# Two transformer mixers on one core: the projections as plain f32 products, without the split into fp32r halves

## The chip, the core and the metric

The kernel runs as one program on one of the eight cores of a Trainium2 chip. The metric is the device time of one execution in microseconds (us), lower being better. A core has four engines that matter here: TensorE (PE; its weight loads are listed apart as PEld), VectorE (DVE), ScalarE (ACT) and GpSimd (POOL). The queue of SyncE (SP) issues the loads from HBM, and 16 DMA engines carry them out.

## What is computed

Two transformer blocks run one after the other on 256 tokens of width 1024, all in f32. Each block is a mixer and then a mixture of experts. Cut to the lines that matter:

```
# block 1
proj = rms_norm(x, g_mix) @ w_in                      # 1024 x 5432
ya = gla_mixer(...) @ w_br_gla ;  yb = dsa_mixer(...) @ w_br_att
x = x + (sigmoid(gate_a) * ya + sigmoid(gate_b) * yb) @ w_out
x = x + hier_moe(rms_norm(x, g_ffn), ...)             # 32 experts, width 128
# block 2
proj = rmsnorm(x, norm_mix_2) @ w_in_2                # 1024 x 3080
x = x + concat(rmsnorm(forgetting), rmsnorm(dilated)) @ w_out_2
x = x + hierarchical_moe(...)                         # 32 experts, width 512
```

The experts are picked by the largest router logits, so the products that feed the routers need more digits than one fp32r product gives.

## The kernel before

**Stages.** Mixer 1 (0 to about 228 us) is followed by routing and experts of block 1 (to about 338 us), mixer 2 (to about 490 us) and the experts of block 2 (to the end at 959.4 us). The 256 tokens are two tiles of 128 (`NT = 2`, `tt`). Activations are turned to 128 features by 256 tokens once for each mixer (`to_feat`, L325).

**Weights.** Every weight tile is 128 x 4096 f32, 2 MB, loaded by SP into one of several slots (`wload`, `stream_tile`). A slot is filled again when its last reader is done. Five slots exist from the start and others are opened as memory comes free; the experts have 9 in block 1 and 10 in block 2. So the first 9 or 10 expert tiles can be loaded ahead of the routing, and no more.

**Projections.** `project` (L298) loads 1024 rows of up to 512 columns and calls `gemm_tok` (L280): for each of 8 steps of 128 rows (`k`) it multiplies both token tiles with that slice of weights, into an accumulator `acc` (PSUM, 4 banks). `gemm_feat` (L290) does the same the other way round for the four gate projections: the weights stand in the array and the 256 tokens stream, four products a step. `mixed` (L737), `out_step` (L752) and `out_part` (L1222) are the output projections.

**The split.** Each operand x of such a product is held as two fp32r tiles, hi = x rounded to fp32r and lo = x - hi. `split` (L252) makes both for a slice of weights: ACT writes hi (`whi`, L263), then DVE or POOL in turn writes lo (`wlo`, L264). `products` (L267) issues three matmuls for each product: hi*hi, hi*lo, lo*hi, all of them on L269. The activations' halves are made where they are turned: `to_feat` (L325: `aT_hi` by ACT, `aT_lo` by DVE), `feat_split` (L374), and L749/L750 in `mixed`.

```
with tc.high_priority(offset=SPLIT_AHEAD):
    turn[1] = nc.scalar.activation(r[0], v, AF.Copy)
    eng.tensor_sub(r[1], v, r[0].bitcast(F32))
```

**Order.** No order is written out by hand: a list scheduler places the instructions on each engine by their dependences and priorities, and each engine then runs its list strictly in that order. `SPLIT_AHEAD` raises the priority of the splits. A later projection's matmuls are placed between an attention's matmuls where the scheduler sees a gap.

**Other names.** `head_norm` (L345) normalizes the heads of a projection (ACT L343 and L351, DVE L352, L307 to L313, L355). `pairs_T` (L358) turns them by transposes on PE (L365) and scales on DVE (L369, L371). `rope` (L1124) comes between the two in mixer 2 (POOL L1132, DVE L1134, L1135). L436 and L443 are transposes and products of attention. L571 is a plain f32 product of 128x128 with 128x512, called four times; L623 is one of 128x128 with 128x256, called twice. L541 to L551 find each token's 64 largest index scores on DVE (the mask chain). In names such as `b`, `t4` tiles are meant.

Of the kernel before, what the change touches and what calls it, by code (L numbers as in the profile page):

```python
# [20 lines left out]
P = 128  # L21
T = 256
# [6 lines left out]
SPLIT_AHEAD = 30  # L29
SPLIT_ENGINES = ('vp', 'pv')  # L30
# [106 lines left out]
def two_blocks(ctx: ExitStack, tc: tile.TileContext, A: dict, at: dict, out: bass.AP):  # L137
# [112 lines left out]
    turn = [0, None, 0]  # L250

    def split(v):  # L252
        n = 1
        for c in v.shape[1:]:
            n *= c
        r = []
        for tag in ("whi", "wlo"):
            t = wtile([P, 512], F32R, tag=tag, bufs=4)[:, :n]
            r.append(t if len(v.shape) == 2 else t.rearrange("p (k n) -> p k n", n=v.shape[2]))
        turn[0] += 1  # L260
        eng = nc.gpsimd if SPLIT_ENGINES[turn[2]][turn[0] % 2] == "p" else nc.vector
        with tc.high_priority(offset=SPLIT_AHEAD):
            turn[1] = nc.scalar.activation(r[0], v, AF.Copy)  # L263
            eng.tensor_sub(r[1], v, r[0].bitcast(F32))  # L264
        return r

    def products(todo):  # L267
        def mm(out_, a, b, start, stop, kw):
            nc.tensor.matmul(out_, a, b, start=start, stop=stop, **kw)  # L269

        for out_, (ah, al), (bh, bl), split_a, first, last, kw in todo:
            mm(out_, ah, bh, first, False, kw)
            mm(out_, *((ah, bl) if split_a else (al, bh)), False, False, kw)
        for out_, (ah, al), (bh, bl), split_a, first, last, kw in todo:
            mm(out_, *((al, bh) if split_a else (ah, bl)), False, last, kw)

# [3 lines left out]
    def gemm_tok(ws, hT, accs, then=None):  # L280
        for k in range(8):
            if then is not None and k == then[0]:
                with tc.issue_after(turn[1].ins):
                    then[1]()
            for w, ac in zip(ws, accs):
                wh, wl = split(w[:, k, :])
                products([(ac[tt][:, :w.shape[2]], [h[:, k, tok(tt)] for h in hT], (wh, wl), False, k == 0, k == 7, {})
                          for tt in range(NT)])

    def gemm_feat(w, hT, accs):  # L290
        for k in range(8):
            wh, wl = split(w[:, k, :])
            sl = [slice(b * P, (b + 1) * P) for b in range(4)]
            products([(accs[b // 2][:, (b % 2) * T:(b % 2 + 1) * T], (wh[:, sl[b]], wl[:, sl[b]]),
                       [h[:, k, :] for h in hT], True, k == 0 and b % 2 == 0, k == 7, {"skip_group_check": True})
                      for b in range(4)])

    def project(src, c0, ns, hT, then=None, step=8):  # L298
        ws = [wload(src, 0, 8, c0 + sum(ns[:i]), n, step) for i, n in enumerate(ns)]
        ac = [[acc() for _ in range(NT)] for _ in ns]  # L300
        gemm_tok(ws, hT, ac, then)
        return ac if len(ns) > 1 else ac[0]
# [22 lines left out]
    def to_feat(g):  # L325
        hi = wtile([P, 8, T], F32R, tag="aT_hi", bufs=1, level="inner")
        lo = wtile([P, 8, T], F32R, tag="aT_lo", bufs=1, level="inner")
# [12 lines left out]
        return hi, lo  # L340
# [33 lines left out]
    def feat_split(src, dst, tt, g):  # L374
# [4 lines left out]
        h, l = (d[:, :, tok(tt)] for d in dst)  # L379
        if g is None:  # L380
            nc.scalar.activation(h, v, AF.Copy)
            nc.vector.tensor_sub(l, v, h.bitcast(F32))
        elif g.shape[1] == 1:
            scaled(h, v, g)
            nc.vector.scalar_tensor_tensor(l, v, g, h.bitcast(F32), op0=OP.mult, op1=OP.subtract)
        else:
            for k in range(4):
                gk = g[:, k:k + 1]
                scaled(h[:, k], v[:, k], gk)
                nc.vector.scalar_tensor_tensor(l[:, k], v[:, k], gk, h[:, k].bitcast(F32),  # L390
                                               op0=OP.mult, op1=OP.subtract)
# [117 lines left out]
    gemm_tok([w], hT, [a2], (5, lambda: token_rstd(r_)))  # L509
# [160 lines left out]
    glaT = [t4([P, 4, T], F32R) for _ in range(2)]  # L670
# [39 lines left out]
    for c in range(4):  # L710
# [16 lines left out]
    mh, ml = stream_tile(F32R).rearrange("p (i k t) -> i p k t", i=2, k=8)  # L727
# [9 lines left out]
    def mixed(b):  # L737
        ps = bank()
        s = slice(b * P, (b + 1) * P)
        for i, (w, src) in enumerate(((wg, glaT), (wa, attT))):  # L740
            wh, wl = split(w[:, :, s])
            products([(ps[:, i * T:(i + 1) * T], (wh[:, k, :], wl[:, k, :]), [x[:, k, :] for x in src],
                       True, k == 0, k == 3, {}) for k in range(4)])
        mm = wtile([P, 2, T], tag="on", bufs=2, level="const")
        m = mm[:, 0]
# [356 lines left out]
    turn[2] = 1  # L1102
# [35 lines left out]
    kb = project(w_in2, 2048, [512], hT, (3, lambda: token_rstd(r_)), 4)  # L1138
# [15 lines left out]
    dilT = [t4([P, 4, T], F32R) for _ in range(2)]  # L1154
    dss = wtile([P, NT], tag="dss", bufs=2)

    def out_branch(on, dst, ss, tt, g):
        junk = wtile([P, 512], tag="sq", bufs=2, level="const")
        feat_split(on, dst, tt, g)
# [59 lines left out]
    foxT = [wtile([P, 4, T], F32R, tag="foxT", bufs=2) for _ in range(2)]  # L1219
    fss = wtile([P, NT], tag="dss", bufs=2)  # L1220

    def out_part(w, src, tts):  # L1222
        xo = {(tt, c): acc() for tt in tts for c in range(2)}
        for c in range(2):
            for k in range(4):
                wh, wl = split(w[:, k, c * 512:(c + 1) * 512])
                products([(xo[tt, c], [x[:, k, tok(tt)] for x in src], (wh, wl), False, k == 0, k == 3, {})
                          for tt in tts])
# [51 lines left out]
```

## Time and profile before

| | |
|---|---|
| three timed runs | 960.49, 962.53 (median), 964.93 us |
| span of the profiled execution (first to last instruction) | 959.4 us |
| PE, PEld busy | 754.1, 477.6 us |
| DVE, ACT, POOL busy | 367.8, 271.9, 170.5 us |
| moved by DMA | 304.69 MB, mean 318 GB/s |
| splits of weights: ACT L263, POOL L264, DVE L264 | 120.0, 134.3, 80.8 us busy |

The profiled execution is a run of its own and its own device time isn't given beside its span; the median of the timed runs lies 3.1 us above the span, which is the work around the first and the last instruction. PE's busy time is no measure of a rate, since matmuls are pipelined: one recorded as 0.39 us may be followed by the next 0.23 us later. So prices are taken from starts, not from durations.

### The profile page before, as it was taken

How to read it: one execution, taken by the hardware profiler on the slowest of the kernel's cores; microseconds unless marked ns; L12 is line 12 of the kernel's file. 1: busy time of each engine (PE TensorE's matmuls, PEld its weight loads, DVE VectorE, ACT ScalarE, POOL GpSimd, SP SyncE). 2: the span in 40 equal slices, each digit the busy share in tenths (PEclk: the TensorE clock that was granted, in tenths of full speed). 3: DMA queues.
4: the chain of work that ended last, by engine and by line, in shares of the span. 5: the costliest groups of instructions: out<-in, count | busy, mean ns of one | idle time of the engine just before them, and what ended most of it. 6: DMA issues, size and time to landing. Idle time of an engine off the chain costs nothing. (4 is left out here: it accounts for less than half of the span.)

```text
span 959.4 us, 13937 instructions
## 1 busy us (share of the span) xinstructions
PE 754.1 (79%) x5662; PEld 477.6 (50%) x5662; DVE 367.8 (38%) x788; ACT 271.9 (28%) x617; POOL 170.5 (18%) x158
## 2 busy tenths in 40 slices
PE   7999999998979997988999756555566585655565
PEld 6778899976657576676863313111222141221212
DVE  4966374565435488676561102010010020100201
ACT  6556555552111274665641000000000000000000
POOL 3422344571000056322420000000000000000001
PEclk9899999999989999999999989889787878898967
DMA  9663453684999983624669999999999999999997
GB/s 342 228 225 130 150 192 146 264 350 177 362 406 409 380 305 104 254 89 180 234 252 411 409 409 410 409 409 409 357 409 410 409 409 410 409 409 409 409 382 240
DMA packets 97782, 304.69 MB, mean 318 GB/s; under 512 B 2920, under 2 KB 19048, under 8 KB 97712
## 3 DMA queue, kind: packets, MB, share of 16 engines
q1 hardware_dynamic: 97136, 302.68, 81.6%
q8 instruction: 48, 0.79, 0.3%
q0 software_dynamic: 288, 0.79, 0.2%
q10 hardware_dynamic: 288, 0.26, 0.1%
q14 instruction: 22, 0.18, 0.1%
HBM read 302.65 MB, written 1.06 MB: 317 GB/s over the span
## 5 line engine op out<-in xcount | busy, mean ns | idle before, releaser
L1079 PE MATMUL acc<-w,XT 128*32 128x128 f32 (+1 forms) x2048 | 185.6, 492 | 85.1 <-DMA w<-w_up 47.4
L264 POOL TENSOR_TENSOR wlo<-w,whi 128x512 fp32r<-128x512 f32 (+3 forms) x104 | 134.3, 1295 | 193.5 <-ACT whi L263 156.2
L1079 PEld LDWEIGHTS acc<-w,XT 128*32 128x32 f32 x2048 | 58.4, 115 | 184.0 <-issue 91.3
L1028 PE MATMUL acc<-w,pT 128*32 128x512 f32 (+1 forms) x712 | 100.5, 681 | 62.0 <-DMA w<-w_down 60.9
L263 ACT ACTIVATE whi<-w 128x512 fp32r<-128x512 f32 (+3 forms) x208 | 120.0, 591 | 81.7 <-PE acc L269 74.3
L264 DVE TENSOR_TENSOR wlo<-w,whi 128x512 fp32r<-128x512 f32 (+3 forms) x104 | 80.8, 781 | 53.7 <-ACT whi L263 51.0
L1000 DVE TENSOR_TENSOR on<-acc,sq 128x512 fp32r<-128x512 f32 (+1 forms) x35 | 22.5, 645 | 201.2 <-ACT sq L999 200.8
L269 PE MATMUL acc<-whi,aT_hi 128*128 128x512 f32 (+3 forms) x240 | 90.4, 382 | 1.4 <-ACT b L343 0.7
L269 PE MATMUL acc<-whi,aT_lo 128*128 128x512 f32 (+3 forms) x240 | 88.4, 373 | 0.0
L1028 PEld LDWEIGHTS acc<-w,pT 128*32 128x32 f32 x712 | 22.8, 123 | 129.3 <-DMA w<-w_down 78.0
L1008 POOL DMA_DIRECT2D out<-X x6 | 3.4, 574 | 457.5 <-DVE X L1006 457.5
L269 PE MATMUL acc<-wlo,aT_hi 128*128 128x512 f32 (+3 forms) x240 | 70.6, 375 | 3.5 <-POOL wlo L264 3.5
L999 ACT ACTIVATE sq<-acc 128x512 fp32r<-128x512 f32 (+1 forms) x35 | 19.5, 560 | 187.9 <-PE acc L1028 187.9
L1012 DVE SCALAR_TENSOR_TENSOR on<-acc,sc,sq 128x128 f32<-128x128 f32 (+1 forms) x16 | 11.6, 723 | 132.1 <-PE acc L1079 131.2
L1022 ACT ACTIVATE pT<-ps 128x128 f32<-128x128 f32 (+1 forms) x16 | 7.0, 437 | 193.8 <-PE ps L1020 193.8
L269 PEld LDWEIGHTS acc<-whi,aT_hi 128*128 128x128 f32 x240 | 47.7, 199 | 11.3 <-ACT b L343 1.8
L269 PEld LDWEIGHTS acc<-whi,aT_lo 128*128 128x128 f32 x240 | 47.7, 199 | 7.3 <-issue 0.9
L269 PEld LDWEIGHTS acc<-wlo,aT_hi 128*128 128x128 f32 x240 | 44.3, 198 | 11.2 <-POOL wlo L264 4.1
L989 ACT ACTIVATE ST<-ps 128x256 fp32r<-128x256 f32 x16 | 6.1, 383 | 133.2 <-PE ps L986 133.2
L974 PE MATMUL ps<-S,H 128*128 128x128 f32 x256 | 38.4, 309 | 5.5 <-PEq L913 3.6
L1006 DVE TENSOR_TENSOR X<-X,ps 128x512 f32<-128x512 f32 (+1 forms) x70 | 40.5, 635 | 4.9 <-PE ps L1004 4.6
L974 PEld LDWEIGHTS ps<-S,H 128*128 128x128 f32 x256 | 35.1, 218 | 12.0 <-issue 10.2
(277 smaller groups left out, 1084.3 us busy)
## 6 DMA issues: line engine op xcount, KB each, us to landing
w<-w_up SPq DMA_DIRECT2D x40, 2048.0 KB, 23.7
w<-w_gate SPq DMA_DIRECT2D x40, 2048.0 KB, 23.6
w<-w_down SPq DMA_DIRECT2D x35, 2048.0 KB, 23.6
w<-w_in SPq DMA_DIRECT2D x13, 2048.0 KB, 10.6
w<-w_down SPq DMA_DIRECT2D x18, 512.0 KB, 10.4
w<-w_out SPq DMA_DIRECT2D x4, 2048.0 KB, 8.2
w<-w_in SPq DMA_DIRECT2D x2, 1056.0 KB, 16.8
w<-w_in SPq DMA_DIRECT2D x2, 1040.0 KB, 14.9
```

What stands on the lines that cost most here:

```text
L263: turn[1] = nc.scalar.activation(r[0], v, AF.Copy)
L264: eng.tensor_sub(r[1], v, r[0].bitcast(F32))
L269: nc.tensor.matmul(out_, a, b, start=start, stop=stop, **kw)
L974: nc.tensor.matmul(ps[:, kk * n:(kk + 1) * n], h[:, tt, kp + kk, :], S[:, tt].rearrange("p e s -> p (e s)"), start=i == 0, stop=i == len(t ...
L989: nc.scalar.activation(ST, ps[:, :T], AF.Copy)
L999: nc.scalar.activation(yh, yp[:, :n], AF.Copy)
L1000: nc.vector.tensor_sub(yl, yp[:, :n], yh.bitcast(F32))
L1006: nc.vector.tensor_add(xs, xs, ps[:, :n])
L1012: nc.vector.scalar_tensor_tensor(hid.rearrange("s c p -> s p c"), gu[1][:, :F].rearrange("s (p c) -> s p c", c=n2), sc[:, 1:2], sg[:, :F]. ...
L1022: nc.scalar.activation(t[:, :n2].rearrange("p c s -> p (c s)"), ps[:, :F], AF.Copy)
L1028: nc.tensor.matmul(yp[js], hT_[:, c, js], w, start=c == 0, stop=c == n2 - 1)
L1079: mm = nc.tensor.matmul(gu[i][32 * j:32 * j + 32, :F], XT[k * gn // 8][:, k % (8 // gn), (g % gn) * P + 32 * j:(g % gn) * P + 32 * j + 32] ...
```

## The change

The split is gone. `split`, `products` and the halves `whi`, `wlo`, `aT_hi`, `aT_lo`, `mh`, `ml` no longer exist; each product is one matmul call on f32 operands, the weights straight from the slot that the DMA filled. The turned activations are single f32 tiles (`aT`, `mT`, `attT`, `glaT`, `dilT`, `foxT`); `feat_split` becomes `to_rows` with one operation. `mT` has a tile of its own, where `mh` and `ml` took a stream slot for a while. `token_rstd` is issued ahead of the first projection of a mixer instead of within it. The experts and routers are as before. The diff, cut to its core:

```
     def gemm_tok(ws, hT, accs):
         for k in range(8):
             for w, ac in zip(ws, accs):
-                wh, wl = split(w[:, k, :])
-                products([(ac[tt][:, :w.shape[2]], [h[:, k, tok(tt)] for h in hT], (wh, wl), False, k == 0, k == 7, {})
-                          for tt in range(NT)])
+                for tt in range(NT):
+                    nc.tensor.matmul(ac[tt][:, :w.shape[2]], hT[:, k, tok(tt)], w[:, k, :], start=k == 0, stop=k == 7)
 
     def gemm_feat(w, hT, accs):
         for k in range(8):
+            for b in range(4):
+                nc.tensor.matmul(accs[b // 2][:, (b % 2) * T:(b % 2 + 1) * T], w[:, k, b * P:(b + 1) * P], hT[:, k, :],
+                                 start=k == 0 and b % 2 == 0, stop=k == 7, skip_group_check=True)
...
     def to_feat(g):
-            for kk in range(2):
-                k = kp + kk
-                s = ps[:, kk * T:(kk + 1) * T]
-                nc.scalar.activation(hi[:, k, :], s, AF.Copy, scale=g[:, k:k + 1])
-                nc.vector.scalar_tensor_tensor(lo[:, k, :], s, g[:, k:k + 1], hi[:, k, :].bitcast(F32),
-                                               op0=OP.mult, op1=OP.subtract)
-        return hi, lo
+            nc.scalar.activation(hT[:, kp, :], ps[:, :T], AF.Copy, scale=g[:, kp:kp + 1])
+            nc.vector.tensor_scalar_mul(hT[:, kp + 1, :], ps[:, T:], g[:, kp + 1:kp + 2])
+        return hT
...
     def mixed(b):
-            wh, wl = split(w[:, :, s])
-            products([(ps[:, i * T:(i + 1) * T], (wh[:, k, :], wl[:, k, :]), [x[:, k, :] for x in src],
-                       True, k == 0, k == 3, {}) for k in range(4)])
+            for k in range(4):
+                nc.tensor.matmul(ps[:, i * T:(i + 1) * T], w[:, k, s], src[:, k, :], start=k == 0, stop=k == 3)
...
-        nc.gpsimd.tensor_add(m, m, mm[:, 1])
-        nc.scalar.activation(mh[:, b], m, AF.Copy)
-        nc.vector.tensor_sub(ml[:, b], m, mh[:, b].bitcast(F32))
+        nc.gpsimd.tensor_add(mT[:, b], mm[:, 0], mm[:, 1])
 
     def out_step(c, b, xo):
-        wh, wl = split(wo[c][:, b, :])
-        products([(xo[tt], (mh[:, b, tok(tt)], ml[:, b, tok(tt)]), (wh, wl), False, b == 0, b == 7, {})
-                  for tt in range(NT)])
+        for tt in range(NT):
+            nc.tensor.matmul(xo[tt], mT[:, b, tok(tt)], wo[c][:, b, :], start=b == 0, stop=b == 7)
```

The scheduler places the rest anew. On PE at the start of mixer 2, before, the end of the second projection (`qb`, 128x512), the transposes of the first one's rotated heads (L365) and the start of the third projection (128x260):

```order
L269 MATMUL acc<-whi,aT_hi 128x512
L269 MATMUL acc<-whi,aT_lo 128x512
L269 MATMUL acc<-wlo,aT_hi 128x512 x2
L269 MATMUL acc<-whi,aT_hi 128x512
L269 MATMUL acc<-whi,aT_lo 128x512
L269 MATMUL acc<-whi,aT_hi 128x512
L269 MATMUL acc<-whi,aT_lo 128x512
L269 MATMUL acc<-wlo,aT_hi 128x512 x2
L365 MATMUL ps<-zk,b_4137 128x128 x8
L269 MATMUL acc<-whi,aT_hi 128x260
```

The same place in the change (L255 is the product of `gemm_tok`, L296 the transposes of `to_feat`, L325 those of `pairs_T`, L360 the scores):

```order
L296 MATMUL ps<-zk,X 128x128
L255 MATMUL acc<-w,aT 128x512
L296 MATMUL ps<-zk,X 128x128 x8
L255 MATMUL acc<-w,aT 128x512 x31
L325 MATMUL ps<-zk,b_2817 128x128 x8
L255 MATMUL acc<-w,aT 128x260 x32
L325 MATMUL ps<-zk,b_2889 128x128 x8
L255 MATMUL acc<-w,aT 128x512
```

Two whole projections still stand ahead of the first transposes, and the whole third one ahead of the second.

On PE later in mixer 2, the change puts seven products (and the small products of the forget gate) between the last transposes of the dilated attention (L337) and the transposes of the forgetting attention's keys, and sixteen more ahead of those of its queries:

```order
L337 MATMUL ps<-zk,on 128x128 x4
L1123 MATMUL ps<-lf,m_2716 128x8
L1124 MATMUL ps<-lf,m_2716 128x8
L1125 MATMUL ps<-lf,ones 128x8
L1129 MATMUL ps<-m_2716,lf 8x128
L1130 MATMUL ps<-m_2716,lf 8x128
L1131 MATMUL ps<-ones,lf 8x128
L255 MATMUL acc<-w,aT 128x512 x7
L325 MATMUL ps<-zk,b_3176 128x128 x8
L255 MATMUL acc<-w,aT 128x512 x16
L325 MATMUL ps<-zk,b_3230 128x128 x8
```

Before, 35 of the fp32r matmuls stood where the seven products stand, and 25 where the sixteen stand.

On DVE in mixer 1, the end of the mask chain, before (L352 and L307 belong to the norm of the first projection's heads, `wlo` is a split):

```order
L548 MAX m_361<-score 128x8
L264 TENSOR_TENSOR wlo<-w,whi 128x512
L549 MATCH_REPLACE score<-m_361,score 128x256
L548 MAX m_364<-score 128x8
L549 MATCH_REPLACE score<-m_364,score 128x256
L352 TENSOR_REDUCE hss<-sq 128x8
L548 MAX m_367<-score 128x8
L352 TENSOR_REDUCE hss<-sq 128x8
```

and in the change:

```order
L504 MATCH_REPLACE score<-m_297,score 128x256
L503 MAX m_300<-score 128x8
L504 MATCH_REPLACE score<-m_300,score 128x256
L506 TENSOR_SCALAR selmask<-score 128x256
L312 TENSOR_REDUCE hss<-sq 128x8
L513 COPY sq<-ps 8x512
```

The mask chain now ends ahead of the norm, and nothing of a split stands in it.

## Rows read from the trace of the kernel before

**Rows 1.** The page: span, PE's busy tenths and DMA's, in 40 slices.

```profile
span 959.4 us, 13937 instructions
...
PE   7999999998979997988999756555566585655565
...
DMA  9663453684999983624669999999999999999997
```

**Rows 2.** Busy by stage: start:end, length, engines, granted clock, DMA share, GB/s.

```profile
0.00:228.00 228.00, 215.77 (x1413) 187.88 (x1414) 137.30 (x270) 127.69 (x266) 99.83 (x90) 0.99 0.62 228
338.00:490.00 152.00, 137.68 (x780) 112.59 (x781) 110.36 (x202) 95.14 (x245) 64.73 (x55) 0.97 0.51 192
...
235.00:240.00 5.00, 5.00 (x81) 4.19 (x80) 2.79 (x5) 0.00 (x0) 0.00 (x0) 1.00 0.02 5
...
500.00:959.40 459.40, 293.12 (x1970) 103.11 (x1968) 58.58 (x136) 23.23 (x42) 3.43 (x6) 0.85 1.00 396
```

**Rows 3.** Timeline of PE: start us, length us; fp32r steps of two products, 512 wide.

```profile
111.96 0.39 PE L269 MATMUL acc<-whi,aT_hi 128*128 128x512 f32 x1
...
113.32 0.39 PE L269 MATMUL acc<-whi,aT_hi 128*128 128x512 f32 x1
...
342.84 0.40 PE L269 MATMUL acc<-whi,aT_hi 128*128 128x512 f32 x1
...
344.24 0.40 PE L269 MATMUL acc<-whi,aT_hi 128*128 128x512 f32 x1
```

**Rows 4.** The plain f32 product of L571: its records, and PEld's timeline there.

```profile
L571 PE MATMUL ps<-b,m x8: 592/592/595, 60.1 to 63.1; 128*128 128x512 f32 x8
...
60.48 0.19 PEld L571 LDWEIGHTS ps<-b,m 128*128 128x128 f32 x1 [0.24 <-PE ps L365]
...
62.63 0.19 PEld L571 LDWEIGHTS ps<-b,m 128*128 128x128 f32 x1 [0.24 <-issue]
```

**Rows 5.** Timeline of PE: fp32r steps of four products, 256 wide; f32 ones (L623).

```profile
142.79 0.64 PE L269 MATMUL acc<-aT_hi,wlo 128*128 128x256 f32 x4
...
144.23 0.64 PE L269 MATMUL acc<-aT_hi,wlo 128*128 128x256 f32 x4
...
108.42 1.03 PE L623 MATMUL ps<-la,m 128*128 128x256 f32 x4
109.28 0.95 PE L636 MATMUL ps<-m,la 128*128 128x2 f32 x8
```

**Rows 6.** Timeline of PE: fp32r steps of two products, 264 wide.

```profile
71.71 0.28 PE L269 MATMUL acc<-whi,aT_hi 128*128 128x264 f32 x1
...
72.43 0.28 PE L269 MATMUL acc<-whi,aT_hi 128*128 128x264 f32 x1
```

**Rows 7.** PE's waits in mixer 2, then mixer 1: who, us in total, times, longest.

```profile
PE acc L269 <- POOL wlo L264: 3.5, 2, 3.2
PE ps L365 <- DVE b L1135: 2.7, 2, 1.5
PE ps L365 <- DVE b L355: 2.5, 1, 2.5
...
PE ps L365 <- DVE b L355: 1.9, 2, 1.7
...
PE acc L269 <- POOL wlo L264: 0.6, 1, 0.6
```

**Rows 8.** The page: the groups of the weights' splits, busy us and mean ns.

```profile
L264 POOL TENSOR_TENSOR wlo<-w,whi 128x512 fp32r<-128x512 f32 (+3 forms) x104 | 134.3, 1295 | 193.5 <-ACT whi L263 156.2
...
L263 ACT ACTIVATE whi<-w 128x512 fp32r<-128x512 f32 (+3 forms) x208 | 120.0, 591 | 81.7 <-PE acc L269 74.3
L264 DVE TENSOR_TENSOR wlo<-w,whi 128x512 fp32r<-128x512 f32 (+3 forms) x104 | 80.8, 781 | 53.7 <-ACT whi L263 51.0
```

**Rows 9.** Timelines of DVE and POOL ahead of the queries' transposes in mixer 1.

```profile
56.07 0.18 DVE L311 TENSOR_TENSOR rs_t<-rs_t,rs_v 128x16 f32<-128x16 f32 x1
...
56.49 1.25 DVE L313 TENSOR_TENSOR rs_y<-rs_y,rs_t 128x16 f32<-128x16 f32 x1
...
56.43 1.28 POOL L264 TENSOR_TENSOR wlo<-w,whi 128x512 fp32r<-128x512 f32 x1 [1.85 <-ACT whi L263]
```

More of the change, by code (lines that the diff above doesn't have):

```diff
@@ L248, in wload @@
         return v
[L250 to L275, printed above, removed]
     def tok(tt):
@@ L278, in tok, with gemm_tok @@
         return slice(tt * P, (tt + 1) * P)
-    def gemm_tok(ws, hT, accs, then=None):
+    def gemm_tok(ws, hT, accs):
         for k in range(8):
-            if then is not None and k == then[0]:
-                with tc.issue_after(turn[1].ins):
-                    then[1]()
             for w, ac in zip(ws, accs):
-                wh, wl = split(w[:, k, :])
-                products([(ac[tt][:, :w.shape[2]], [h[:, k, tok(tt)] for h in hT], (wh, wl), False, k == 0, k == 7, {})
-                          for tt in range(NT)])
+                for tt in range(NT):
+                    nc.tensor.matmul(ac[tt][:, :w.shape[2]], hT[:, k, tok(tt)], w[:, k, :], start=k == 0, stop=k == 7)
@@ L290, in gemm_feat @@
     def gemm_feat(w, hT, accs):
         for k in range(8):
[L292 to L298, printed above, removed]
+            for b in range(4):
+                nc.tensor.matmul(accs[b // 2][:, (b % 2) * T:(b % 2 + 1) * T], w[:, k, b * P:(b + 1) * P], hT[:, k, :],
+                                 start=k == 0 and b % 2 == 0, stop=k == 7, skip_group_check=True)
@@ L299, in project @@
+    def project(src, c0, ns, hT, step=8):
         ws = [wload(src, 0, 8, c0 + sum(ns[:i]), n, step) for i, n in enumerate(ns)]
         ac = [[acc() for _ in range(NT)] for _ in ns]
-        gemm_tok(ws, hT, ac, then)
+        gemm_tok(ws, hT, ac)
         return ac if len(ns) > 1 else ac[0]
@@ L325, in to_feat @@
     def to_feat(g):
-        hi = wtile([P, 8, T], F32R, tag="aT_hi", bufs=1, level="inner")
-        lo = wtile([P, 8, T], F32R, tag="aT_lo", bufs=1, level="inner")
+        hT = wtile([P, 8, T], tag="aT", bufs=1, level="inner")
         for kp in range(0, 8, 2):
@@ L378, in feat_split @@
         v = ps.rearrange("p (k t) -> p k t", k=4)
-        h, l = (d[:, :, tok(tt)] for d in dst)
+        d = dst[:, :, tok(tt)]
         if g is None:
-            nc.scalar.activation(h, v, AF.Copy)
-            nc.vector.tensor_sub(l, v, h.bitcast(F32))
+            nc.scalar.activation(d, v, AF.Copy)
         elif g.shape[1] == 1:
-            scaled(h, v, g)
-            nc.vector.scalar_tensor_tensor(l, v, g, h.bitcast(F32), op0=OP.mult, op1=OP.subtract)
-        else:
[L387 to L391, printed above, removed]
+            scaled(d, v, g)
+        else:
+            nc.vector.tensor_mul(d, v, g[:, :, None].to_broadcast([P, 4, P]))
     def scores(tt, qT, kT, add_psum, add_sbuf, expo):
@@ L588, in two_blocks @@
         scaled(vb[:, tt, :], a2[tt], rstd[:, tt:tt + 1])
-    attT = [t4([P, 4, T], F32R) for _ in range(2)]
+    attT = t4([P, 4, T])
     for tt in range(NT):
         on = values(scores(tt, qTd, kTd, add_sel, add_rel, neg_max), vb)
-        feat_split(on, attT, tt, None)
+        to_rows(on, attT, tt, None)
     ar = project(w_in, GLA_R, [264, 264], hT)
@@ L669, in two_blocks @@
                                                u[:, pair * P:(pair + 1) * P], op0=OP.mult, op1=OP.add)
-    glaT = [t4([P, 4, T], F32R) for _ in range(2)]
+    glaT = t4([P, 4, T])
     O = [bank() for _ in range(2)]
@@ L1153, in two_blocks @@
         scaled(vd[:, tt, :260], av[0][tt][:, :260], r)
-    dilT = [t4([P, 4, T], F32R) for _ in range(2)]
+    dilT = t4([P, 4, T])
     dss = wtile([P, NT], tag="dss", bufs=2)
@@ L1218, in two_blocks @@
     open_stream(2, 3)
-    foxT = [wtile([P, 4, T], F32R, tag="foxT", bufs=2) for _ in range(2)]
+    foxT = wtile([P, 4, T], tag="foxT", bufs=1)
     fss = wtile([P, NT], tag="dss", bufs=2)
@@ L1225, in out_part @@
             for k in range(4):
-                wh, wl = split(w[:, k, c * 512:(c + 1) * 512])
-                products([(xo[tt, c], [x[:, k, tok(tt)] for x in src], (wh, wl), False, k == 0, k == 3, {})
-                          for tt in tts])
+                for tt in tts:
+                    nc.tensor.matmul(xo[tt, c], src[:, k, tok(tt)], w[:, k, c * 512:(c + 1) * 512],
+                                     start=k == 0, stop=k == 3)
         return xo
```

18 lines of the change are left out of this document (8 added, 10 removed).

## The prediction

> **What bounds the kernel now.** I read the page's 40 slices first [rows 1]. They show two kinds of stage. In slices 11 to 14 and 22 to 39 DMA stands at 9 throughout, and from slice 23 on PE falls to 5 to 8: the experts wait for their weights. In the rest, the two mixers, DMA has many slices of 2 to 6 and PE is at 7 to 9, mostly 9. The table by stage says the same in numbers [rows 2]: in mixer 1 (0 to 228 us) PE is busy for 215.77 of 228 us with the DMA share at 0.62, in mixer 2 (338 to 490 us) for 137.68 of 152 us with DMA at 0.51, and from 500 us to the end DMA stands at 1.00.
>
> So two questions decide. Does the time of a mixer follow PE? It nearly must: the idle time is 228 - 215.77 = 12.2 us and 152 - 137.68 = 14.3 us, 26.5 in all, and that is the most that any relief of the other engines could return. Does the end of the kernel follow the mixers? Between 235 and 240 us DMA runs at a share of 0.02 [rows 2]: the nine expert slots are full, and loads begin again only when the experts free one. A later routing therefore can't be made up by loads done meanwhile; the expert stages start later and take as long as before. The same holds for the ten slots of block 2. The added `mT` tile changes nothing in that number.
>
> **The price of a product.** In fp32r a step of two products 512 wide is six matmuls. From the start of one step to the start of the next it takes 113.32 - 111.96 = 1.36 us in mixer 1 and 344.24 - 342.84 = 1.40 us in mixer 2 [rows 3]; I take 1.38. A plain f32 product is in this trace too: L571 is called four times and has eight records, so a product is two records [rows 4]. Their weight loads start at 60.48 and, five records later, at 62.63 us: 2.15 / 5 = 0.43 us a record, 0.86 us a product. A step of two products takes 1.72 us, 0.34 more. The loads themselves last 0.19 us and lie inside the record before [rows 4].
>
> At 256 columns a step of four products takes 144.23 - 142.79 = 1.44 us in fp32r [rows 5]. L623, called twice, has four f32 records of this shape; the next instruction starts 109.28 - 108.42 = 0.86 us after the first, so a record costs 0.215 us, and four products 8 x 0.215 = 1.72 us, 0.28 more. At 264 columns a step of two products takes 72.43 - 71.71 = 0.72 us [rows 6]; in f32 I scale the 256-wide record to 0.215 x 264 / 256 = 0.222 us, four of them 0.89, 0.17 more (260 columns are taken as 264).
>
> **The sum on PE.** The counts are the loops of the code.
>
> - 512 wide: ten projections of 8 steps, 16 steps of `out_step`, 16 of `out_part`, 112 in all: 112 x 0.34 = 38.1 us.
> - 256 wide: four gate projections of 8 steps, and 64 products of `mixed`, which are 16 such steps: 48 x 0.28 = 13.4 us.
> - 264 and 260 wide: 16 steps in each mixer: 32 x 0.17 = 5.4 us.
> - 296 wide: 8 steps, no f32 row of this shape; between the 0.17 and the 0.34 I take 0.2: 1.6 us.
>
> Together +58.5 us, some 37 in mixer 1 and 21.5 in mixer 2. All of it lies on PE, the engine that both mixers wait for.
>
> **What comes back.** The split's work goes: 120.0 us on ACT, 134.3 on POOL, 80.8 on DVE [rows 8], and the second half of each turned activation. None of these engines sets the mixers' time by itself, so their hours count for nothing; what counts is the part of PE's waits that ends. From [rows 7], for mixer 2 and then mixer 1:
>
> - PE waits 3.5 us for `wlo` on POOL, and 0.6 in mixer 1. These waits can't occur any more: -4.1.
> - 2.7 us for the rotated heads (L1135). Their cover, the second projection, grows from 8 x 1.40 = 11.2 to 8 x 1.72 = 13.8 us, and the chain loses the splits that stood between its steps: -2.7.
> - 2.5 us for the forgetting attention's keys (L355). In the new order seven products cover that chain, 7 x 0.86 = 6.0 us against 35 matmuls at 1.40 / 6, 8.2 us. The cover shrinks while the chain gets shorter: I give -1.0.
> - 1.9 us for the heads in mixer 1 (L355): a chain that was held up by a split (below): -1.2.
>
> That is 9.0 us. About 1 us more comes from the clock: the mean of 0.97 in mixer 2 [rows 2] contains stretches at the lower level, 1.2 GHz, and fewer waits leave fewer of them. No wait is added by the code. The DVE order has the whole mask chain ahead of the first norm, but that norm is wanted only after the next projection, 13.8 us later. A slot is now held until its last matmul and not until its last split; DMA has the room for that at shares of 0.62 and 0.51 [rows 2]. Both cost nothing as long as that cover holds; if a projection did wait for weights, a 2 MB tile at the 396 GB/s of [rows 2] would cost some 5 us.
>
> **Sum:** 58.5 - 9.0 - 1.0 = +48.5 us. On the profiled execution that is a span of 959.4 + 48.5 = 1007.9 us [rows 1]; against the median of the runs, 962.53 (3.1 above that span), 1011 us.
>
> **A rule weighed.** In the chain of the 1.9 us wait, DVE's L313 on 128x16 elements took 1.25 us, from 56.49, while its like L311 took 0.18; POOL worked on a split from 56.43 for 1.28 us, and DVE came free with it [rows 9]. By that row alone one chain loses 1.1 us, which I have counted. The Trainium skill, "SBUF — State Buffer", section "SBUF: two separate sides", says that DVE with two SBUF inputs and GpSimd share a port pair under an exclusive lock, so that the later one waits for the whole instruction of the other. By that rule all 104 POOL splits could hold up a chain, and what comes back would be nearer to all the idle time, which is the second rival's sum. The trace agrees with the rule at this place; how often it held a chain that PE waited for, the rows don't show.
>
> **The rivals.**
>
> *Nothing comes back.* The chains keep PE waiting at other places, since the scheduler now leaves fewer and larger pieces between an attention's matmuls. For it: the waits on attention's own work (L436, L443 and the like) make up much of the idle time, and seven products in place of 35 matmuls is less cover. Against it: the 4.1 us of waits for `wlo` have no successor. It gives 962.5 + 58.5 = 1021 us, and up to 1026 with a new wait of 5 us.
>
> *All comes back.* Every idle microsecond of the mixers was the splits' doing: 58.5 - 26.5, and 2 us for the clock: 962.5 + 30 = 993 us. Against it: the first microseconds are a wait for the first loads, and the waits named in [rows 7] add up to 11.2 us.
>
> *The other side: an f32 product is one record.* If each product took one record and not two, a step of 512 would fall from 1.38 to 0.86 us, one of 256 from 1.44 to 0.86, one of 264 from 0.72 to 0.44: 112 x 0.52 + 48 x 0.58 + 32 x 0.28 = 95 us less on PE, about 870 us. The place is every product, and it decides at once: with one record the change gains, with two it loses. Against it stands the eight-for-four of [rows 4]. The Trainium skill, "Perfetto Trace Analysis", section "Engine Utilization", gives the array's output rate as halved for FP32_LOW_HIGH; read as the whole price it would mean one such record a product. The trace disagrees: the halved rate is that of one record, and there are two.
>
> *It is hidden.* If loads done during the longer mixers shortened the expert stages, the time would stay at 962 us. The idle DMA at 235 us with all slots full speaks against it.
>
> **The numbers.** Forecast 0.74; nothing comes back, or a new wait, 0.14; all comes back 0.08; hidden 0.02; one record 0.02. "Faster" and "slower" mean by more than 0.5%, 4.8 us, about what a measurement here can tell. Slower has 0.96, same 0.02, faster 0.02. The range leaves out the far end of either rival: from 1000 us (two thirds of the idle time back: 58.5 - 18 - 3 = +37.5) to 1021 us (nothing back).
>
> **What would show it.** Right: L255 with two records for each call, 0.43 us apart at 512 columns; a mixer 1 that ends some 34 to 37 us later and a mixer 2 that is some 12 to 16 us longer; no wait on a split; POOL nearly idle in the mixers; expert stages as long as before with DMA at 1.00. Wrong: f32 records closer than 0.43 us or farther apart at 256 columns because of their weight loads; PE idle for over 26 us in the mixers; or DMA idle in the expert stages.

## The result, and the profile after

The changed kernel takes 990.38 us (median of 4 runs, 988.40 to 992.17), the kernel before 961.51 us beside it: a ratio of 1.030, with a 95% interval of 1.027 to 1.033, or +28.9 us. The forecast was +48.5 us. The direction was right, the size was not: 1011 us was forecast, and the range began at 1000. The profiled execution took 989.29 us with a span of 987.5 us, 1.8 us more than its span; the 3.1 us that stand ahead of the prediction for this difference came from two different executions.

The page of the kernel after answers to [rows 1]; the PEclk line is the granted clock in tenths:

```profile
span 987.5 us, 12141 instructions
...
PE   7999999999897989999999957657656566565655
...
PEclk9999999999998999999999977777788888888887
DMA  9841737417399959933277999999999999999997
```

Products first. PE's timeline answers to [rows 3] and [rows 5] (start us, length us):

```profile
22.70 14.00 PE L255 MATMUL acc<-w,aT 128*128 128x512 f32 x32
36.63 1.02 PE L512 MATMUL ps<-b,m 32*8 32x512 f32 x2
...
163.99 27.79 PE L260 MATMUL acc<-aT,w 128*128 128x256 f32 x128
191.62 0.59 PE L697 MATMUL ps<-b,w 128*128 128x256 f32 x2
```

The 16 products of a projection 512 wide are 32 records; from the first one's start to the next instruction's it takes 36.63 - 22.70 = 13.93 us, 0.435 us a record. At 256 columns 128 records take 191.62 - 163.99 = 27.63 us, 0.216 each. That is the price of the forecast, two records a product.

So the difference lies in what came back. The stages by window answer to [rows 2] (start:end, length, then PE, PEld, DVE, ACT and POOL busy, granted clock, DMA share, GB/s): mixer 1, mixer 2, a stretch of the first expert stage, the last stages:

```profile
0.00:253.20 253.20, 246.17 (x1057) 165.57 (x1058) 71.61 (x188) 55.48 (x124) 15.45 (x25) 1.00 0.56 202
363.80:519.80 156.00, 153.18 (x647) 88.79 (x646) 67.94 (x150) 49.25 (x146) 12.59 (x20) 1.00 0.61 223
265.00:270.00 5.00, 5.00 (x109) 4.25 (x110) 1.73 (x5) 0.57 (x2) 0.00 (x0) 1.00 0.06 9
530.00:987.50 457.50, 296.64 (x1968) 100.30 (x1960) 58.32 (x136) 23.24 (x42) 3.42 (x6) 0.83 1.01 397
```

For a like cut of the kernel before, each mixer is taken from its start (the second one from its first transposes, L332) to the first filler matmul of its routing (L233). Windows of the kernel before, and then the stretches in it at the lower clock:

```profile
0.00:227.00 227.00, 214.77 (x1408) 187.36 (x1409) 136.84 (x268) 127.06 (x264) 98.96 (x89) 0.98 0.62 227
336.60:489.70 153.10, 138.69 (x790) 113.49 (x789) 111.11 (x204) 96.26 (x244) 64.73 (x55) 0.97 0.52 193
...
23.70:30.50 6.80, 6.80 (x22) 4.92 (x17) 6.63 (x22) 2.84 (x5) 1.46 (x1) 0.51 1.07 372
378.50:381.50 3.00, 2.73 (x12) 2.67 (x13) 2.90 (x4) 1.05 (x2) 2.49 (x4) 0.50 0.00 0
429.70:433.00 3.30, 3.30 (x9) 2.56 (x8) 3.27 (x5) 0.63 (x1) 1.19 (x1) 0.50 0.00 0
453.50:456.50 3.00, 3.00 (x16) 3.00 (x17) 0.69 (x1) 2.04 (x4) 0.00 (x0) 0.51 1.02 418
```

Mixer 1 grew from 227.0 to 253.2 us, mixer 2 from 153.1 to 156.0, together +29.1 us; the first expert stage grew by 1.0, what follows mixer 2 (469.7 us, then 467.7) shrank by 2.0. The mixers' 29.1 us are three terms. PE's **idle time** fell from 12.2 + 14.4 to 7.0 + 2.8 us: -16.8. The **clock** stood at 0.5 (1.2 of 2.4 GHz) for 17 us of the mixers before, in these four stretches (windows of half a microsecond add up to 6.8 and 10.2 us), and in no window of the mixers after; PE is busy in nearly all of that time at half its pace, so I estimate that they cost 8.5 us: -8.5. The **rest**, busy time without the clock's loss, grew from 345.0 to 399.4 us: +54.4. Each of these numbers is from one execution.

PE's waits after, mixer 1 and then mixer 2, answer to [rows 7]:

```profile
PE ps L296 <- DMA zk<-zk: 4.6, 1, 4.6
PE ps L390 <- ACT b L376: 0.8, 1, 0.8
PE ps L296 <- DMA X<-x: 0.7, 1, 0.7
...
PE ps L325 <- DVE b L315: 1.0, 2, 0.7
PE ps L1146 <- ACT b L376: 0.7, 1, 0.7
```

The waits for the first loads are all that is left of any length. There is no wait for a low half, for rotated heads, or for attention's values. The last one stood in mixer 2 before, next to those of [rows 7]:

```profile
PE ps L443 <- ACT b L343: 1.8, 1, 1.8
```

### The profile page after: what moved, and what is told of

Its sections match the earlier page's. It is cut to its first block, busy times and chain, and to the rows that moved or that the text cites. A ratio compares the mean times of both kernels' runs of the same rounds, so it can differ in the third digit from the quotient of the medians.

```text
span 987.5 us, 12141 instructions
## 1 busy us (share of the span) xinstructions
PE 806.2 (82%) x5166; PEld 430.5 (44%) x5166; DVE 259.3 (26%) x652; ACT 152.8 (15%) x377; POOL 33.2 (3%) x54
## 5 line engine op out<-in xcount | busy, mean ns | idle before, releaser
L255 PE MATMUL acc<-w,aT 128*128 128x512 f32 (+3 forms) x480 | 182.3, 530 | 0.2 <-ACT aT L298 0.2
L255 PEld LDWEIGHTS acc<-w,aT 128*128 128x128 f32 x480 | 88.9, 192 | 75.1 <-issue 68.0
L260 PE MATMUL acc<-aT,w 128*128 128x256 f32 x256 | 55.8, 379 | 0.0
L260 PEld LDWEIGHTS acc<-aT,w 128*128 128x128 f32 x256 | 48.5, 190 | 6.7 <-issue 0.2
L927 DVE TENSOR_TENSOR XT<-ps,ck 128x256 f32<-128x256 f32 (+1 forms) x48 | 24.6, 513 | 32.6 <-PE ps L924 32.5
L303 ACT ACTIVATE b<-acc,rs_y 128x512 f32<-128x512 f32 (+5 forms) x28 | 16.6, 608 | 81.6 <-PE acc L255 69.9
L705 PE MATMUL acc<-w,mT 128*128 128x512 f32 x64 | 28.5, 595 | 0.0
L697 PE MATMUL ps<-b,w 128*128 128x256 f32 x128 | 27.8, 379 | 0.0
L954 PE MATMUL ps<-sq,ST 128*128 128x512 f32 (+1 forms) x70 | 23.9, 419 | 2.9 <-ACT sq L949 2.9
L697 PEld LDWEIGHTS ps<-b,w 128*128 128x128 f32 x128 | 24.3, 190 | 3.3
```

Of the source, the lines that this page charges most:

```text
L255: nc.tensor.matmul(ac[tt][:, :w.shape[2]], hT[:, k, tok(tt)], w[:, k, :], start=k == 0, stop=k == 7)
L260: nc.tensor.matmul(accs[b // 2][:, (b % 2) * T:(b % 2 + 1) * T], w[:, k, b * P:(b + 1) * P], hT[:, k, :], start=k == 0 and b % 2 == 0, sto ...
L697: nc.tensor.matmul(ps[:, i * T:(i + 1) * T], w[:, k, s], src[:, k, :], start=k == 0, stop=k == 3)
L705: nc.tensor.matmul(xo[tt], mT[:, b, tok(tt)], wo[c][:, b, :], start=b == 0, stop=b == 7)
L927: nc.vector.tensor_mul(XT[kp * gn // 8][:, k:k + 2, :], ps[:, :2 * n].rearrange("p (k s) -> p k s", k=2), gI[:, kp:kp + 2, None].to_broadc ...
L954: nc.tensor.matmul(ps[:, :n], ST[:, tok(tt)], y, start=i == 0, stop=i == 1)
```

## The experiments

Two theories; the diffs below are cut to their core. **A**: the split's work on the weights was what kept PE waiting, so it comes back whenever that work goes. **B**: the longer plain products are what covers the chains. Three kernels set the work and the products apart.

| kernel | median us | ratio to before (95%) | mixer 1, us | mixer 2, us |
|---|---|---|---|---|
| before | 961.5 | 1 | 227.0 | 153.1 |
| after | 990.4 | 1.030 (1.027 to 1.033) | 253.2 | 156.0 |
| e1 three passes, no low halves | 935.3 | 0.973 (0.971 to 0.974) | 218.5 | 136.0 |
| e2 three passes, no split at all | not read | | 219.0 | 139.0 |
| e3 plain, with copies | 1007.6 | 1.050 (1.047 to 1.053) | 258.1 | 170.0 |
| e4 mixer 2 alone plain | 963.1 | 1.002 (1.001 to 1.003) | 227.8 | 155.9 |
| e5 low halves on DVE | 949.4 | 0.986 (0.984 to 0.989) | 224.7 | 142.7 |
| e6 = e1 + POOL scratch | 945.9 | 0.985 (0.982 to 0.988) | 225.8 | 137.7 |
| e7 = e1 + DVE scratch | 941.7 | 0.979 (0.977 to 0.980) | 221.2 | 140.7 |
| e8 = e5, splits earlier | 951.0 | 0.989 (0.986 to 0.991) | 227.6 | 143.8 |
| e9 filler in one wait | 957.1 | 0.997 (0.995 to 0.998) | 226.0 | 149.2 |
| e10 = after + POOL scratch | 993.0 | 1.032 (1.029 to 1.035) | 257.3 | 156.8 |
| e11 one projection off POOL | 955.5 | 0.994 (0.992 to 0.996) | 225.5 | 148.5 |
| e12 POOL for outputs only | 947.1 | 0.985 (0.983 to 0.988) | 221.9 | 143.5 |

The mixers' lengths are those of the profiled execution, cut as above.

**e1, three passes without the low halves' work** (`zero(n)` is a resident tile of zeros).

```diff
-        eng = nc.gpsimd if SPLIT_ENGINES[turn[2]][turn[0] % 2] == "p" else nc.vector
+        lo = zero(n)
         with tc.high_priority(offset=SPLIT_AHEAD):
             turn[1] = nc.scalar.activation(hi, v, AF.Copy)
-            eng.tensor_sub(r[1], v, r[0].bitcast(F32))
```

> The kernel before with its three passes, but the weights' low half is a tile of zeros: DVE and POOL split no weight any more, ACT still copies the high half (the weights' low part is left out of the result). Theory A, the relief in the changed kernel came from the split's work that is gone, and most of it from the low halves on POOL and DVE: PE loses most of its waits and the half-clock stretches behind them, mixer 1 ends 5 to 9 us earlier, mixer 2 is 8 to 13 us shorter, 940 to 950 us. Theory B, the relief came from the longer plain products, which keep PE fed while the chains run: three passes keep their waits except the 4.1 us for wlo, 955 to 962 us.

Measured 935.3 us, 26.2 less, below the range that A gave. With the same number of matmuls PE is idle for 8.8 and 3.3 us in place of 12.2 and 14.4 (windows of e1):

```profile
0.00:218.50 218.50, 209.75 (x1408) 184.34 (x1409) 78.66 (x204) 129.00 (x264) 17.89 (x29) 0.98 0.65 236
327.80:463.80 136.00, 132.70 (x791) 109.43 (x790) 70.67 (x164) 95.62 (x246) 11.37 (x14) 1.00 0.60 224
```

Three passes don't need long waits. Theory B falls: the shorter products cover the chains as well, once the low halves are gone. The zeros make no product cheaper: a step of two, 512 wide, takes 33.34 - 31.98 = 1.36 us in e1, as before [rows 3].

PE's busy time fell too. Without the clock's loss (6.8 us at half the clock in mixer 1) it is 209.75 + 132.70 - 3.4 = 339.0 us, 5.9 less than the 345.0 of the kernel before for the same matmuls. So before, some 6 us of slower work stood in what the profile calls busy, and went away with the low halves. Some 1.6 of them, by the starts, are in the first projection (296 wide): its matmuls start 0.25 us apart until 13 us in the kernel before, and 0.14 us apart from 8 us on in e1.

**e2, no split of weights at all** (`fixed` holds one pair of halves per mixer, made from its first chunk).

```diff
-            turn[1] = nc.scalar.activation(r[0], v, AF.Copy)
-            eng.tensor_sub(r[1], v, r[0].bitcast(F32))
+        hi, lo = (t[:, :n] for t in fixed[turn[2]])
```

> The kernel before with its three passes, but every product reads one resident pair of halves made once per mixer (all the other weights are left out of the result; routing is then that of other numbers, so the mixers' stages are what is read): no weight is split anywhere, the turned activations are still split. Theory A: the most relief that three passes can have, mixer 1 ends 8 to 12 us earlier and mixer 2 is 10 to 15 us shorter than before, about 935 to 943 us. Theory B: the waits of attention stay, 953 to 960 us. If this is faster than the first run by over 4 us, ACT's copies matter too; if by less than 2 us, they don't.

Its routing is that of other numbers, and its first expert stage alone took 760.6 us, so its total says nothing. Its mixers took 219.0 and 139.0 us, no less than e1's. So nothing shows here that ACT's 208 copies, 120.0 us on the page [rows 8], cost time; e6 below has a place where one of them does.

**e3, plain products with the weights' work left in.** In `copies`, ACT copies the chunk, and DVE or POOL in turn subtracts zeros from that copy:

```diff
+                c = copies(w[:, k, :])
                 for tt in range(NT):
-                    nc.tensor.matmul(ac[tt][:, :w.shape[2]], hT[:, k, tok(tt)], w[:, k, :], start=k == 0, stop=k == 7)
+                    nc.tensor.matmul(ac[tt][:, :w.shape[2]], hT[:, k, tok(tt)], c[tt], start=k == 0, stop=k == 7)
```

> The changed kernel with its plain products, but the split's work is kept on the weights: ACT copies each chunk, DVE or POOL makes a second copy from it by a subtraction of zeros, and the products read the two copies in turn. Theory A: the relief goes away with the work back, 1003 to 1018 us, and PE waits again in both mixers for 15 to 25 us. Theory B: 988 to 995 us, since the longer products cover the copies as well.

Measured 1007.6 us, 17.2 above the kernel after; 14.0 of it in mixer 2, where PE is idle for 12.8 us in place of 2.8:

```profile
367.00:537.00 170.00, 157.19 (x647) 89.55 (x646) 104.99 (x190) 91.03 (x226) 60.62 (x56) 0.99 0.49 180
```

In mixer 1 PE is idle for 8.5 us (7.0 after), so the waits came back almost only in mixer 2. A holds on this side too, though its share is smaller than with three passes.

**e4, mixer 1 as before, mixer 2 plain.**

```diff
+PLAIN = (False, True)
...
+        if PLAIN[turn[2]]:
+            return v, v
...
+                mm(out_, a[0], b[0], first, last, kw)
```

> Mixer 1 as before, with halves and three passes; mixer 2 as changed, plain. If the two mixers' prices add up: the mixer 2 of the changed kernel was 2.9 us longer than that of before, so 963 to 967 us. If what mixer 2 got back depends on the state that mixer 1 left: up to 975 us.

963.1 us, with a mixer 2 of 155.9 us, as in the kernel after: the two mixers' prices add up. In mixer 2 what came back pays for the plain products almost whole; in mixer 1 it doesn't.

**e5, all low halves on DVE.**

```diff
-SPLIT_ENGINES = ('vp', 'pv')
+SPLIT_ENGINES = ('vv', 'vv')
```

> The kernel before with every low half on DVE and none on POOL. The first two runs say that the low halves cost the three-pass kernel 8.5 us in mixer 1 and 17 us in mixer 2, and that ACT's copies cost next to nothing. Theory A1, it is POOL: slow splits that products wait for, and POOL's work that makes DVE's instructions longer; without it 943 to 953 us, DVE's own 512-wide splits near 0.6 us and no 1.25 us instruction on 16 elements. Theory A2, it is DVE's queue: with twice the splits in it the chains come later still, 965 to 985 us.

949.4 us: faster than both kernels. A1's time holds, A2 falls, and the whole computation is done. DVE's group of subtractions shows why twice as many fit:

```profile
L264 DVE TENSOR_TENSOR wlo<-w,whi 128x512 fp32r<-128x512 f32 (+3 forms) x208 | 135.1, 666 | 42.5 <-ACT whi L263 39.3 <-PE acc L269 2.4
```

One takes 666 ns where it took 781 beside POOL's [rows 8]. Mixer 2 is 10.4 us shorter, mixer 1 only 2.3. A half-clock stretch that it has at 214 us costs it 1.7 us there.

**e6 and e7, the subtractions of POOL or of DVE alone, into scratch that nothing reads** (against e1; `junk` is the scratch tile, shown without its reshaping; e7 has `!= "p"` and `nc.vector`).

```diff
             turn[1] = nc.scalar.activation(hi, v, AF.Copy)
+            if SPLIT_ENGINES[turn[2]][turn[0] % 2] == "p":
+                nc.gpsimd.tensor_sub(junk, v, v)
```

> The first run's kernel (three passes, zeros for the low halves), with POOL's half of the subtractions put back into scratch tiles that nothing reads (the weights' low part is left out of the result): no product waits for POOL, only POOL's occupation of its path to SBUF is back. Theory A1 (POOL's work lengthens DVE's): 943 to 955 us, with long DVE instructions beside POOL's. Theory A1' (only the waits for POOL's late tiles count): 935 to 938 us.

> The same with DVE's half of the subtractions put back into scratch tiles, and none on POOL (the weights' low part is left out of the result). Theory A2 (DVE's queue): 943 to 955 us. Theory A1: 936 to 941 us, since DVE has room for 100 short subtractions when POOL is idle.

945.9 and 941.7 us. e6 is in the range of A1, and A1' falls; e7 lies between the ranges that its two theories gave. Against e1's 935.3, POOL's half costs 10.6 us and DVE's 6.4, and what DVE does beside POOL becomes longer. Windows of e6:

```profile
0.00:225.80 225.80, 210.17 (x1408) 184.31 (x1409) 86.10 (x204) 128.82 (x264) 79.78 (x93) 0.98 0.62 228
335.30:473.00 137.70, 132.81 (x790) 109.32 (x789) 76.74 (x164) 95.92 (x245) 48.86 (x54) 1.00 0.59 220
```

The same 204 and 164 DVE instructions as in e1 take 86.10 + 76.74 us in place of 78.66 + 70.67, 13.5 more. One group shows it at its plainest, the sum of the index scores (groups of DVE, busy and mean ns; e1, then e6):

```profile
L549 DVE SCALAR_TENSOR_TENSOR score<-b,wi,score 128x128 f32<-128x128 f32 (+1 forms) x14 | 5.7, 406 | 0.5
```

```profile
L553 DVE SCALAR_TENSOR_TENSOR score<-b,wi,score 128x128 f32<-128x128 f32 (+1 forms) x14 | 11.3, 810 | 0.5
```

Of the 8.5 us between the two profiled executions (942.0 and 933.5 us), 5.2 are one wait in mixer 1. ACT's timeline in e6, then PE's:

```profile
47.80 0.21 ACT L318 ACTIVATE rs_y<-rs_v 128x16 f32<-128x16 f32 x1 [9.65 <-DVE rs_v L317]
47.93 0.61 ACT L270 ACTIVATE whi<-w 128x512 fp32r<-128x512 f32 x1
```

```profile
48.59 0.79 PE L279 MATMUL acc<-whi,aT_hi 128*128 128x512 f32 x1 [5.22 <-ACT whi L270]
```

A high half stood in ACT's queue behind a step of the queries' norm, which waited 9.65 us for DVE; PE waited for the copy. In e1 ACT's queue has the same order, and PE doesn't wait there. What differs is how long DVE's chain ahead of that step takes. DVE's first index score in e1, ACT's step in e1, and DVE's first index score in e6:

```profile
20.64 0.29 DVE L547 TENSOR_SCALAR score<-b,wi 128x128 f32<-128x128 f32 x1 [2.50 <-ACT b L543]
41.35 0.22 ACT L314 ACTIVATE rs_y<-rs_v 128x16 f32<-128x16 f32 x1 [2.37 <-DVE rs_v L313]
```

```profile
21.22 0.29 DVE L551 TENSOR_SCALAR score<-b,wi 128x128 f32<-128x128 f32 x1 [2.20 <-ACT b L547]
```

From the first score to ACT's step it is 20.7 us in e1 and 26.6 in e6, 5.9 more, and the sum of the scores alone is 5.6 of them. So this wait is POOL's lengthening of DVE's instructions, carried to PE by ACT's queue: worked off in order, it held a product up for a chain that the product doesn't need.

**e8, e5 with the splits moved farther ahead.**

```diff
-SPLIT_AHEAD = 30
+SPLIT_AHEAD = 60
```

> The kernel with all low halves on DVE (949.35 us), and the splits moved twice as far ahead in the scheduler's priorities (60 in place of 30). If products still wait for low halves that come late, 944 to 948 us; if the splits then stand ahead of attention's own chains in DVE's queue, 950 to 956 us.

951.0 us; its interval overlaps that of e5. No gain shows, and neither reading is decided.

**e9, matmuls in the wait.** The largest wait in mixer 2 has the same form as that in e6. POOL's timeline before, and PE's:

```profile
373.77 4.25 POOL L1132 TENSOR_TENSOR sq<-b,ropeS 128x256 f32<-128x256 f32 x4 [1.16 <-DVE b L355]
377.99 2.75 POOL L264 TENSOR_TENSOR wlo<-w,whi 128x260 fp32r<-128x260 f32 x3
```

```profile
378.77 0.80 PE L269 MATMUL acc<-wlo,aT_hi 128*128 128x260 f32 x2 [3.24 <-POOL wlo L264]
```

The low half stood behind four products of the rotation. The half-clock stretch follows. e9 leaves the wait and fills it:

```diff
             mm(out_, *((ah, bl) if split_a else (al, bh)), False, False, kw)
+        if turn[2] == 1 and calls[1] == 28:
+            ps = bank()
+            for _ in range(12):
+                tc.keep_in_program_order(
+                    nc.tensor.matmul(ps, ones_b, ones_b[:, None, :].to_broadcast([P, 4, P]), start=True, stop=True))
```

> The kernel before with twelve bf16 matmuls of 512 columns (0.22 us each by the groups of L233), whose result nothing reads, put on PE between the products at which it waits 3.24 us for a low half on POOL (375.5 to 378.8 us); the wait's end stays where it was. Theory: the half-clock stretch right behind that wait is due to PE's idling, so it goes, mixer 2 is 1.7 us shorter and the time 959 to 961 us. Rival: the clock falls there anyway (it is due to something else), no change within 0.5 us, or up to 0.5 us slower.

957.1 us over 12 runs, 4.1 less: more than the theory's 1.7 us, and outside both forecasts. PE's timeline and window of e9:

```profile
375.28 2.76 PE L280 MATMUL ps<-ones_b 128*128 128x512 bf16 x12
378.70 0.51 PE L270 MATMUL acc<-wlo,aT_hi 128*128 128x260 f32 x2 [0.66 <-POOL wlo L265]
```

```profile
378.50:381.50 3.00, 2.36 (x17) 2.15 (x18) 3.00 (x4) 1.33 (x3) 2.44 (x4) 1.00 0.00 0
```

The wait ended where it did (378.70 for 378.77), the clock stayed at 1.00, and mixer 2 lost 3.9 us. For the stretch behind this wait that speaks for the theory and against the rival, in the one execution that was profiled. The rest of the gain is two later stretches that are missing too, and their waits weren't filled (last section).

**e10, the kernel after with POOL's scratch work** (`scratch` gives every second chunk a subtraction on POOL).

```diff
             for w, ac in zip(ws, accs):
+                scratch(w[:, k, :])
                 for tt in range(NT):
```

> The changed kernel with POOL's half of the subtractions put back on its weights, into scratch tiles that nothing reads. With the copies of the third run it was 17.2 us slower than the changed kernel. If POOL's occupation of the path to SBUF and of its own queue (the rope's products) makes up most of that, 996 to 1004 us; if the products' waits for the tiles do, 990 to 994 us.

993.0 us (989.1 to 994.6), 2.7 above the kernel after, whose runs reach from 988.4 to 992.2; 3.4 us of mixer 1's 4.1 are a half-clock stretch of this execution. POOL's work alone takes next to nothing from the plain kernel. By elimination, most of e3's 17.2 us is due to the products' waiting for the copies and to the copies on the other engines; e3 also puts `mT` back into a stream slot, which no run tested alone.

**e11, one projection's low halves off POOL.** Eight subtractions of 208 change their engine:

```diff
-        eng = nc.gpsimd if SPLIT_ENGINES[turn[2]][turn[0] % 2] == "p" else nc.vector
+        pool = SPLIT_ENGINES[turn[2]][turn[0] % 2] == "p" and not (turn[2] == 1 and 16 < calls[1] <= 32)
+        eng = nc.gpsimd if pool else nc.vector
```

> The kernel before, but the low halves of one projection of mixer 2 (the 260-wide values and forgetting logits, 16 chunks, 8 of them on POOL) all on DVE; the other 96 stay on POOL. Theory: the 3.24 us wait is a low half that stands behind the rope's products (L1132, 4.25 us) in POOL's queue; moved out of that queue the wait goes, and the half-clock stretches behind it with it: mixer 2 shorter by 4 to 8 us, 954 to 958 us. Rival: DVE has the same chain in its queue (L355, L1134, L1135) and the low halves come as late from there: 960 to 963 us.

955.5 us, 5.9 less, with mixer 2 at 148.5. What PE waits for in it, in mixer 2:

```profile
PE ps L368 <- DVE b L1138: 4.4, 4, 1.4
PE ps L368 <- DVE b L358: 2.5, 1, 2.5
...
PE acc L272 <- POOL wlo L267: 0.2, 1, 0.2
```

The wait for the low half is down from 3.5 to 0.2 us, and that for the rotated heads rose from 2.7 to 4.4. So the queue was the cause of the 3.24 us. The expectation that the half-clock stretches go with it holds only in part. They are 6.8 us in place of 10.2: the one at 453.5 us is gone, but one still stands where the first did, behind two waits for rotated heads (PE's timeline and window of e11):

```profile
375.45 0.41 PE L368 MATMUL ps<-zk,b 128*128 128x128 f32 x2 [1.43 <-DVE b L1138]
376.67 0.67 PE L368 MATMUL ps<-zk,b 128*128 128x128 f32 x3 [0.81 <-DVE b L1138]
```

```profile
377.00:380.50 3.50, 3.50 (x18) 3.49 (x17) 2.55 (x6) 1.64 (x4) 0.64 (x1) 0.52 0.41 103
```

**e12, POOL for the output stages alone** (`turn[3]` is true in `out_step` and `out_part` only).

```diff
-        eng = nc.gpsimd if SPLIT_ENGINES[turn[2]][turn[0] % 2] == "p" else nc.vector
+        pool = SPLIT_ENGINES[turn[2]][turn[0] % 2] == "p" and turn[3]
+        eng = nc.gpsimd if pool else nc.vector
```

> Low halves on DVE everywhere but in the two output stages (out_step and out_part), where POOL again takes every second one; there no head is normed and POOL has little other work. If POOL does harm only where attention's chains stand in the queues, 945 to 950 us, as fast as with DVE alone or up to 3 us faster; if POOL's work beside DVE's is the harm anywhere, 951 to 956 us.

947.1 us (945.8 to 949.0): as fast as e5 or slightly faster, the intervals overlap. Twenty low halves on POOL (DVE has 188 of the 208) show no harm in these two stages. It is the fastest version here that leaves nothing out, 1.5% under the kernel before and 4.4% under the one after.

## Why the prediction was wrong

**What bounds the kernel: right.** The mixers follow PE, and the expert stages stayed as they were; with all slots full DMA stands at 0.06 between 265 and 270 us, as it did at 0.02 [rows 2].

**The price of a product: right.** Two records each, 0.435 us at 512 columns and 0.216 at 256 against 0.43 and 0.215. The term of +58.5 us came out as +54.4 by busy time. e1 tells why that is too low: the busy time before held 5.9 us that e1 doesn't need for the same matmuls, and against e1's 339.0 us the plain products cost 60.4. The one-record rival falls with the rows of L255.

**What comes back: wrong.** This is the step that failed: "That is 9.0 us. About 1 us more comes from the clock". Measured were 16.8 us of idle time and, by estimate, 8.5 us of clock. The sum is 54.4 - 16.8 - 8.5 = 29.1 us for the mixers. The idle 26.5 us weren't "the most that any relief of the other engines could return" either: the busy time held the clock's loss and the 5.9 us that e1 shows.

- *The waits.* I credited those whose named releaser was a split or a chain in which I had seen one, and let the rest of the 26.6 us stand as attention's own. The 4.1 us for `wlo` and the 2.7 us for rotated heads did go. But of the 4.4 us for normed heads, of which I credited 2.2, only 1.0 is left, and the 1.8 us for values, which I left standing, are gone too. e1 shows that these waits were the low halves' doing: with three passes and the same chains they disappear as well. "The cover shrinks" was the wrong thing to fear; with the splits away the chains end early enough that less cover will do.
- *The clock.* I read a mean of 0.97 in one mixer and gave 1 us. Means of 0.98 and 0.97 over 380 us are 17 us at the lower level, worth some 8.5. How much of it hangs on the waits is open. In mixer 2, 5.1 of them, e9 speaks for the link at the first stretch, 1.7 us: with the wait filled, the clock stayed full. The other two were missing in e9 with their waits in place, and in e11 the 3.24 us wait is gone, but a stretch stands behind others. In mixer 1, 3.4 of them, the low halves aren't the cause: e1, without them, has the same 6.8 us (17.5 to 24.5 us, right behind a wait of 1.8 us for ACT). The kernel before had them 4.7 us after a wait of 0.65 us, and e10, the kernel after with scratch work on POOL, has 6.8 us again (21 to 28 us). Why the one profiled execution of the kernel after has none stays open; it may be chance.

**The rivals.** "All comes back", at 993 us and a chance of 0.08, comes within 3 us of the time, but by other terms than its own, so that its number is luck: 10 of the 26.6 us of idle time stayed (5.3 of them the first loads), and the clock gave 8.5 in place of 2. I held against it that the waits of [rows 7] add up to 11.2 us; a wait's row names the last releaser, not what made that releaser late. "Nothing comes back" and "hidden" fall.

**The rule that was weighed.** POOL's work does make DVE's longer: 13.5 us in e6, and 13.9 in e10, where the kernel after's 188 and 150 DVE instructions take 79.77 + 73.64 us in place of 71.61 + 67.94 us:

```profile
0.00:257.30 257.30, 249.34 (x1056) 167.07 (x1057) 79.77 (x188) 55.41 (x124) 76.02 (x89) 0.99 0.55 199
367.60:524.40 156.80, 153.37 (x646) 88.71 (x644) 73.64 (x150) 49.20 (x146) 49.77 (x60) 1.00 0.60 221
```

The Trainium skill, "SBUF — State Buffer", section "SBUF: two separate sides", gives DVE and GpSimd a shared port pair under an exclusive lock; these rows agree with it. I had read from it that what comes back would be nearer to all the idle time; 16.8 of 26.6 us did. What the longer instructions cost depends on who waits for the chain that they lengthen. In e6 one such chain held up ACT's queue, and with it PE, for 5.2 us. In the plain kernel no product needs a copy of its weights by ACT, and e10 pays 2.7 us in all for the same lengthening. Beside that, PE felt a low half behind a rotation in POOL's queue (3.24 us, e11) and 104 subtractions in DVE's (6.4 us, e7, where waits of 2.3 us for normed and 1.4 us for rotated heads are back).

**Open.** e6's 10.6 us and e7's 6.4 are 17.0 of the 26.2 that e1 gained; whether the other 9.2 are the products' waits for the low halves themselves, or the two parts don't add up, no run tells. Between e12 and e1 lie 12 us, the price of computing the low halves at all. How much of it is DVE's room and how much the order in which the scheduler then places things wasn't separated. Nor was the difference between 17.2 us (e3) and 26.2 us (e1) for about the same work. What the change does besides, one operation for a turned activation in place of two and `token_rstd` issued earlier, was never tested alone.

## What to carry to other kernels

When work is taken off engines that feed the bounding one in order, credit the idle time of the bounding engine and its clock together, and ask of each wait what stood ahead of the releaser in its queue, and what made that late, not only who the releaser was. Test the two halves of such a change apart: here the split's work could be made cheaper (e5, one line, -1.4%) without paying for slower products. An engine that is idle for over half of the time (POOL worked for 98.96 + 64.73 of the mixers' 380 us before) can still be the wrong place for a tile that PE wants soon, if a chain of another purpose is worked off in the same queue.

## What was not expected of the hardware

The clock fell less regularly than the waits. In e9 only the first of three waits was filled; the later ones of 2.5 us (for normed heads) and 1.8 us (for values) stayed as they were, and yet the stretches at half the clock behind them, at 429.7 and 453.5 us before, did not come:

```profile
427.00:431.00 4.00, 3.18 (x18) 2.80 (x19) 3.79 (x6) 1.15 (x2) 0.61 (x1) 1.00 0.00 0
450.00:453.00 3.00, 1.93 (x18) 1.93 (x19) 0.96 (x3) 3.00 (x7) 0.00 (x0) 1.00 1.02 419
```

The same wait can thus be followed by the lower clock in one execution and not in another; the 12 times of e9 spread from 955.6 to 962.4 us. The first stretch of mixer 1 lasted 6.8 us in the execution of the kernel before that is shown here, and 3.4 us (23.0 to 27.0) in that of e9, whose mixer 1 is the same code; e4, with that code too, has none there and 3.4 us from 51.5 us on.
